# A two-layer decoder step on one core: the mixer norm's shift moved into the last down product, pools that wait tile by tile, another division of the down projection

## The chip, the cores and the metric

The kernel runs on one core of a Trainium2 chip. The metric is the device time of one launch in microseconds (us); the kernel before takes 1140.86 us (median of three runs, 1140.83 to 1141.41). Engines are named as the profile names them: PE is the matrix engine (PEld its weight loads, which overlap the products), DVE the vector engine, ACT the scalar engine, POOL the GpSimd engine, SP the engine that only issues transfers. "POOLq", "DVEq" and the like are the instruction queues of these engines. Transfers issued by POOL form a DMA queue of their own.

## The reference

One step of a two-layer decoder, width 1024, for a prompt of 512 rows and 8 sample rows. Layer 0 mixes the rows by sliding-window attention, layer 1 by gated linear attention. Behind each mixer, and behind each feed-forward part, stands a layer norm of ALPHA·x + f(x). Cut to what the change touches:

```python
xp = layer_norm(ALPHA * xp + mp, ln_mix_g[i], ln_mix_b[i])   # mixer norm
fp, cp = conv_ffn(xp, buf0, ffn_w_up[i], ffn_conv_w[i], ffn_conv_b[i], ffn_w_down[i])
xp = layer_norm(ALPHA * xp + fp, ln_ffn_g[i], ln_ffn_b[i])   # ffn norm

def layer_norm(x, g, b):
    mu = mean(x); var = mean((x - mu) ** 2)
    return (x - mu) * rsqrt(var + LN_EPS) * g + b

def conv_ffn(x, buf, w_up, conv_w, conv_b, w_down):
    h = x @ w_up                              # 1024 -> 2 x 2816
    a, u = h[..., :D_FF], h[..., D_FF:]
    ap = concatenate([buf, a], axis=1)
    c = conv_b + sum(conv_w[j] * ap[:, j:j + T] for j in range(3))
    y = (gelu(c) * u) @ w_down                # 2816 -> 1024
    return y, ap[:, T:]
```

## The kernel before

**Data.** Activations are kept transposed: 128 of the 1024 features on the partitions, eight such blocks (KD), the rows of the batch along the free axis. The 520 rows are two groups, a (256 prompt rows) and b (256 prompt rows and the 8 samples). A 32-bit product is made of three products in the reduced 32-bit type: every operand is split into a high and a low half, and high·high, high·low and low·high are summed in PSUM. One "unit" is a weight tile of 128 x 1024 with its halves wh and wl; a unit's product for one group is 24 matmuls.

**Weights.** SP loads a unit into `raw`; ACT rounds it to wh. The low half is made in one of two ways. Either DVE subtracts, wl = raw - wh (L192); or, in `low_by_dma` (L195), ACT writes wl = -wh (L197) and a transfer issued by POOL adds the weights from memory to it (L198). Six slots (WSLOTS) hold wh and wl; a product that is done releases its slot, and the next load is issued there.

**Feed-forward.** The 22 blocks of 128 hidden features (j = 0 to 21) run in two manners. Blocks 0 to 3 are a gate unit and a value unit each (`ffn_gate`, `ffn_value`), group by group. Meanwhile `row_sums` (L445) prepares sums and differences of the groups' rows, and from block 4 on (PAIRED) `ffn_pair` computes gate and value of both groups together by seven half products (named a11, a12, s2, s1, a22, s4, s3) of 12 matmuls each, 84 in all, in "wide" PSUM tiles of two banks, except the first, a11, in a one-bank tile `onep`. DVE recombines the results (L821), convolves, and splits the gated product into hh, hl (hs for group a), the operands of the down projection.

**The mixer norm's shift.** The norm's result is x·g·r + b. The rounded operands xh, xl get the bias at once, but x itself, which the residual needs later, gets it by a pass of its own: `shift` (L439, the instruction is L441) on POOL, one per group and block, 16 per layer. For the mixer norms these passes are issued by `row_sums` and kept in program order; the difference of the sample columns (`tsum`, L483 and L484) is taken from the shifted x behind them. The norm behind the first feed-forward part shifts in the same way, in another place.

**Down.** The hidden blocks are gone through in parts, FF_PARTS: three of 4 blocks by pairs of output blocks between the pairs (`ffn_down2`, 48 matmuls a unit, 16 units in all with the fourth part), each adding onto x, and the last part of six blocks behind the last pair by `ffn_down`, one unit (18 matmuls a group) for each of the eight output blocks. There four "heads" in four PSUM banks first take the five blocks that are ready (60 matmuls), and then the sixth. `ln_chunk` adds each result to x (L322) and begins the following norm: after output block 0, ones x x gives a first mean (`sc`, L328), which DVE and POOL subtract from all blocks (L337); squares and sums are gathered by POOL (L354, L355).

**What sets the order.** The Tile framework schedules all instructions with a model of the engines and issues them in that order on each engine; an engine runs its queue strictly in order. `issue_after` and `keep_in_program_order` are constraints on that schedule. PSUM is switched at the first pair (L813) from the pools mps and acc to one and wide, and back after the last pair; a pool that opens in space that another leaves waits for all of that pool's tiles.

## Time and profile before

| what | value |
|---|---|
| device time, median of 3 | 1140.86 us (1140.83 to 1141.41) |
| profiled execution | 1140.54 us, of which the span (first to last instruction) 1138.8 us |
| PE busy | 1079.0 us, 95% |
| DVE, ACT, POOL busy | 898.1, 655.3, 339.0 us (79, 58, 30%) |
| mean granted clock of PE | 0.982 |

Stages of the span by their times: the attention layer's products up to 187 us; its feed-forward blocks 0 to 3 to about 221.6; the opening of the pairs to 241; the pairs of layer 0 to 486.3; its last down part and norm to 561; the linear attention to about 787.6; blocks 0 to 3 of layer 1 to 817; the opening to 841; the pairs to 1085.9; the last down part, norm and output to the end. In a row of the windows view the columns are: window, its length, then for PE, PEld, DVE, ACT and POOL the busy time with the count of instructions, the granted clock of PE, the busy share of the DMA engines, and GB/s. In the waits view: who waits, for what, us in total, times, longest. In the timeline: start, duration, engine, line and operation, and in brackets an idle time before it with what ended it; a row can stand for several instructions (x7).

### The profile page before, as it was taken

Reading aid. Unit: us, or ns where it says so; the run is one execution under the profiler, and the core shown is the slowest. Engines: PE = TensorE matmul, PEld = TensorE weight load, DVE = VectorE, ACT = ScalarE, POOL = GpSimd, SP = SyncE. Lnnn points to the kernel's source line nnn. Section 1 sums busy time; section 2 is a strip of 40 time slices with the busy share of each in tenths; the row PEclk is TensorE's granted clock in tenths of the full one; section 3 lists DMA queues with packets and bytes.
Section 4 is the critical chain, followed back from the end, with each engine's and each line's share of the span. In section 5 each row is a group of like instructions: output and inputs, shape, how many; then the busy total and the mean of one; then the engine's idle time right before and its main releaser. Section 6 shows DMA issues by size and latency. Waiting matters only on the chain.

```text
span 1138.8 us, 23875 instructions
## 1 busy us (share of the span) xinstructions
PE 1079.0 (95%) x9174; PEld 1044.8 (92%) x9174; DVE 898.1 (79%) x1796; ACT 655.3 (58%) x1307; POOL 339.0 (30%) x567
## 2 busy tenths in 40 slices
PE   8998999799999999999999999998799999999995
PEld 8997898699999999988899899898799999999985
DVE  7897669957888778877867787779978887877866
ACT  5677556755556665535545555456665566566534
POOL 3575574611111111056311100373411111111045
PEclk9999999989999999999899999999999999999998
DMA  7553034657777777332134454444567777777312
GB/s 227 152 179 101 13 100 130 162 149 177 180 181 174 178 174 183 98 95 91 55 108 130 125 187 144 140 123 148 143 154 185 173 181 173 179 185 179 96 49 76
DMA packets 64465, 161.68 MB, mean 142 GB/s; under 512 B 7992, under 2 KB 28512, under 8 KB 64352
## 3 DMA queue, kind: packets, MB, share of 16 engines
q1 hardware_dynamic: 51536, 119.47, 32.9%
q0 software_dynamic: 10656, 38.80, 19.8%
q10 hardware_dynamic: 2160, 1.89, 0.5%
q8 instruction: 72, 1.18, 0.4%
q14 instruction: 41, 0.34, 0.1%
HBM read 147.47 MB, written 8.47 MB: 137 GB/s over the span
## 4 chain that ended last, share of the span: by engine, by line
PE 57%; DVE 12%; DMA 5%; POOL 3%; issue 2%; ACT 2%; SPq 0%; ACTq 0%; DVEq 0%; POOLq 0%
PE widep L295 8%; PE widep L296 8%; PE widep L297 8%; PE widep L885 5%; PE widep L884 5%; PE widep L883 5%; DMA vb<-dv 3%; PE accp L230 3%; PE accp L228 3%; PE accp L232 3%; PE onep L297 1%; PE onep L296 1%; PE onep L295 1%; DVE xs_a L427 1%; POOL x_a L337 1%
## 5 line engine op out<-in xcount | busy, mean ns | idle before, releaser
L300 ACT ACTIVATE wh<-raw 128x1024 fp32r<-128x1024 f32 x72 | 76.6, 1064 | 119.5 <-PE widep L884 84.4
L198 POOL DMA_DIRECT2D wl<-in_w_down x32 | 27.6, 864 | 338.2 <-ACT wl L197 337.8
L186 ACT ACTIVATE wh<-raw 128x1024 fp32r<-128x1024 f32 (+2 forms) x96 | 97.2, 1012 | 53.5 <-PE widep L296 19.1
L228 PE MATMUL accp<-xh_b,wh 128*128 128x264 f32 x400 | 114.6, 287 | 11.8 <-DVE hprod L797 8.7
L295 PE MATMUL widep<-th,wh 128*128 128x264 f32 (+1 forms) x432 | 119.4, 276 | 0.0
L296 PE MATMUL widep<-tl,wh 128*128 128x264 f32 (+1 forms) x432 | 119.4, 276 | 0.0
L297 PE MATMUL widep<-th,wl 128*128 128x264 f32 (+1 forms) x432 | 119.2, 276 | 0.0
L228 PE MATMUL accp<-xs_a,wh 128*128 128x256 f32 x400 | 110.6, 291 | 2.8 <-ACT xs_a L426 1.1
L232 PE MATMUL accp<-xh_b,wl 128*128 128x264 f32 x400 | 112.6, 281 | 0.0
L230 PE MATMUL accp<-xl_b,wh 128*128 128x264 f32 x384 | 108.1, 282 | 0.0
L230 PE MATMUL accp<-xs_a,wh 128*128 128x256 f32 x384 | 105.2, 287 | 0.2
L301 DVE TENSOR_TENSOR wl<-raw,wh 128x1024 fp32r<-128x1024 f32 x72 | 88.0, 1222 | 19.9 <-ACT wh L300 19.9
L228 PEld LDWEIGHTS accp<-xh_b,wh 128*128 128x128 f32 x400 | 76.5, 191 | 14.4 <-DVE hprod L797 9.7
L821 DVE TENSOR_TENSOR merged<-widep,conv 128x528 f32<-128x528 f32 x72 | 37.4, 561 | 65.0 <-PE widep L297 65.0
L228 PEld LDWEIGHTS accp<-xs_a,wh 128*128 128x128 f32 x400 | 79.1, 198 | 4.9 <-ACT xs_a L426 1.3
L295 PEld LDWEIGHTS widep<-th,wh 128*128 128x128 f32 x432 | 82.4, 191 | 0.0
L296 PEld LDWEIGHTS widep<-tl,wh 128*128 128x128 f32 x432 | 82.4, 191 | 0.0
L297 PEld LDWEIGHTS widep<-th,wl 128*128 128x128 f32 x432 | 82.3, 191 | 0.0
L192 DVE TENSOR_TENSOR wl<-raw,wh 128x1024 fp32r<-128x1024 f32 (+3 forms) x64 | 75.3, 1182 | 7.2 <-ACT wh L186 6.6
L295 PE MATMUL widep<-xh_b,wh 128*128 128x264 f32 x288 | 79.6, 276 | 0.0
L296 PE MATMUL widep<-xl_b,wh 128*128 128x264 f32 x288 | 79.5, 276 | 0.0
L297 PE MATMUL widep<-xh_b,wl 128*128 128x264 f32 x288 | 79.5, 276 | 0.0
(420 smaller groups left out, 4282.4 us busy)
## 6 DMA issues: line engine op xcount, KB each, us to landing
raw<-in_w_up SPq DMA_DIRECT2D x88, 512.0 KB, 3.6
wl<-in_w_up POOLq DMA_DIRECT2D x42, 512.0 KB, 6.3
raw<-in_w_down SPq DMA_DIRECT2D x32, 512.0 KB, 4.1
wl<-in_w_down POOLq DMA_DIRECT2D x32, 512.0 KB, 6.3
raw<-in_w_gla SPq DMA_DIRECT2D x24, 512.0 KB, 3.6
raw<-in_w_mix_o SPq DMA_DIRECT2D x16, 512.0 KB, 4.3
raw<-in_w_down SPq DMA_DIRECT2D x16, 384.0 KB, 3.1
qs<-hl SPq DMA_DIRECT2D x64, 64.0 KB, 2.2
```

Of the source, the lines that this page charges most:

```text
L186: nc.scalar.activation(h[:, c], r[:, c], AF.Copy)
L192: nc.vector.tensor_tensor(l[:, c], r[:, c], h[:, c].bitcast(F32), op=ALU.subtract)
L228: nc.tensor.matmul(o, h[:, ks], xh, start=k == 0, stop=False)
L230: nc.tensor.matmul(o, h[:, ks], xl, start=False, stop=False)
L232: nc.tensor.matmul(o, l[:, ks], xh, start=False, stop=not tail and k == nt - 1)
L295: self.nc.tensor.matmul(o, h[:, ks], rh, start=k == 0, stop=False)
L296: self.nc.tensor.matmul(o, h[:, ks], rl, start=False, stop=False)
L297: self.nc.tensor.matmul(o, l[:, ks], rh, start=False, stop=k == KD // 2 - 1)
L300: self.nc.scalar.activation(hi, src, AF.Copy)
L301: self.nc.vector.tensor_tensor(lo, src, hi.bitcast(F32), op=ALU.subtract)
L883: nc.tensor.matmul(o, h[:, ks], rh, start=k == 0, stop=False)
L884: nc.tensor.matmul(o, h[:, ks], rl, start=False, stop=False)
```

## The change

1. **Shift.** In `row_sums` the 16 shifts are gone. A tile `back` holds ALPHA·b, made by one POOL instruction in `ffn_open`, and the last down product's addition to x becomes x + back + ps in one instruction. `tsum` moves ahead of the first sums; since x is unshifted there, the difference of the biases (`step`) is added by two more small instructions.
2. **Pools.** All pools that open and close in the middle of the kernel, in PSUM and in SBUF, wait tile by tile (`reuse_waits="tile"`).
3. **Parts.** The last two parts of FF_PARTS are (12, 14) and (14, 22) in place of (12, 16) and (16, 22). A part of two blocks covers four output blocks per unit, so that a unit is 48 matmuls as before; there are 14 units between the pairs in place of 16, and the pairs 18 to 21 follow each other with none between. The last part has eight blocks: units of 512 KB and 24 matmuls a group.
4. **Last down's low halves.** `ffn_down` joins the units whose low halves are made by ACT and a transfer from POOL's queue.
5. **Heads.** Two heads (FULL) take all three products of the seven ready blocks, two take only the products with wh, and their low products come last. The heads are issued behind the last pair's last matmul.
6. **Order of the first pairs.** a11 of the pairs 4 to 6 is issued behind the last matmul written before it, and in pair 4 the product a22 goes ahead of s1.

The number of matmuls of the whole kernel's products is unchanged by 3 and 5.

```diff
-FF_PARTS = ((0, 4), (4, 8), (8, 12), (12, 16), (16, 22))
+FF_PARTS = ((0, 4), (4, 8), (8, 12), (12, 14), (14, 22))
+ORDERED = 3
+FULL = 2
...
     def open(self, name, bufs=1):
-        cm = self.tc.tile_pool(name=name, bufs=bufs)
+        cm = self.tc.tile_pool(name=name, bufs=bufs, reuse_waits="tile")
...
     def psum(self, name, bufs=1):
-        cm = self.tc.tile_pool(name=name, bufs=bufs, space=PSUM)
+        cm = self.tc.tile_pool(name=name, bufs=bufs, space=PSUM, reuse_waits="tile")
...
-            if self.units[u][2] in (self.ffn_down2, self.ffn_gate, self.ffn_value):
+            if self.units[u][2] in (self.ffn_down2, self.ffn_down, self.ffn_gate, self.ffn_value):
                 self.low_by_dma(l[:, c], h[:, c], src[:, c])
...
         if scaled:
-            nc.vector.tensor_tensor(x[:, m], x[:, m], ps, op=ALU.add)
+            nc.vector.scalar_tensor_tensor(x[:, m], x[:, m], self.back[:, m:m + 1], ps, op0=ALU.add, op1=ALU.add)
...
+        ts = self.pp.tile([P, 2, half, NS], F32, name="tsum")
+        gap = step.unsqueeze(2).broadcast_to([P, half, NS])
+        for q, x, y, op in ((0, lo, hi, ALU.subtract), (1, hi, lo, ALU.add)):
+            v.tensor_tensor(ts[:, q], b.x[:, x, 256:], b.x[:, y, 256:], op=ALU.subtract)
+            v.tensor_tensor(ts[:, q], ts[:, q], gap, op=op)
+            self.split(self.th[q][:, :, :, n:], self.tl[q][:, :, :, n:], even(ts[:, q]))
...
-        for m in (*range(half, KD), *range(half)):
-            yield 1
-            for g in (b, a):
-                self.shift(g, i, m)
-        ts = self.pp.tile([P, 2, half, NS], F32, name="tsum")
-        v.tensor_tensor(ts[:, 0], b.x[:, lo, 256:], b.x[:, hi, 256:], op=ALU.subtract)
-        v.tensor_tensor(ts[:, 1], b.x[:, hi, 256:], b.x[:, lo, 256:], op=ALU.subtract)
-        for q in range(2):
-            self.split(self.th[q][:, :, :, n:], self.tl[q][:, :, :, n:], even(ts[:, q]))
...
+        b0 = C_LNB + 2 * layer * KD
+        g.tensor_scalar(self.back, self.par[:, b0:b0 + KD], ALPHA, 0.0, op0=ALU.mult, op1=ALU.add)
...
-        self.half_product(p1, W["a11"], part(a, lo), n)
+        with self.tc.issue_after(self.final) if j < PAIRED + ORDERED else ExitStack():
+            self.half_product(p1, W["a11"], part(a, lo), n)
...
+        products = [(p[:, 0], W["s1"], t1, m), (p[:, 1], W["a22"], t4, n)]
+        for x in reversed(products) if j == PAIRED else products:
+            self.half_product(*x)
...
-            self.heads = heads[2:] + heads[:2]
-            for i, ps in enumerate(self.heads):
-                self.down_steps(g, u + i, ps, range(end))
+            self.heads = [self.acc.tile([P, 512], F32, name="accp") for _ in range(HEADS)]
+            with self.tc.issue_after(self.final):
+                for i, ps in enumerate(self.heads):
+                    self.down_steps(g, u + i, ps, range(end), range(end) if i < FULL else (), True, False)
         if g.i == 0 and m < HEADS:
             ps = self.heads[m]
-            self.down_steps(g, u, ps, [end])
+            self.down_steps(g, u, ps, [end], [end] if m < FULL else range(end + 1), False, True)
```

How the order on the engines moves, at three places. First POOL's queue at the opening of layer 0's pairs, before the change (aext is the gate's convolution input, nconv_p and sconv the convolution state that is written out):

```order
L198 DMA wl<-in_w_down 128x1024
L441 TENSOR_SCALAR x_b<-x_b,par 128x264
L441 TENSOR_SCALAR x_a<-x_a,par 128x256
...
L304 COPY aext<-hist 128x2
L198 DMA wl<-in_w_up 128x1024
L304 COPY nconv_p<-aext 128x2
```

and with it:

```order
L312 COPY aext<-hist 128x2
L201 DMA wl<-in_w_down 128x1024
L201 DMA wl<-in_w_up 128x1024
L312 COPY nconv_p<-aext 128x2
L312 COPY sconv<-aext 128x8
L500 TENSOR_SCALAR xl_b<-xl_b 128x8x4
```

Between the low halves of the first down unit and those of pair 5's first tile (in_w_up) stood 16 shifts, of which the first two are shown; now nothing stands there.

Second, PE at the same place, before (onep_3606 is a11 of pair 5, whose low half is wl_3345; accp_3349 is the last value product; widep_3428 is a12 of pair 4):

```order
L230 MATMUL accp_3349<-xl_b_90,wh_3019 128x264
L232 MATMUL accp_3349<-xh_b_89,wl_3020 128x264
L295 MATMUL onep_3606<-xs_a_86,wh_3344 128x256
L296 MATMUL onep_3606<-xs_a_86,wh_3344 128x256
L297 MATMUL onep_3606<-xs_a_86,wl_3345 128x256
...
L295 MATMUL widep_3428<-xs_a_86,wh_3096 128x256
L296 MATMUL widep_3428<-xs_a_86,wh_3096 128x256
L297 MATMUL widep_3428<-xs_a_86,wl_3097 128x256
```

and with the change (accp_3337 is the last value product, onep_3401 a11 of pair 4, widep_3416 its a12):

```order
L233 MATMUL accp_3337<-xl_b_91,wh_3030 128x264
L235 MATMUL accp_3337<-xh_b_90,wl_3031 128x264
L303 MATMUL onep_3401<-xs_a_87,wh_3103 128x256
L304 MATMUL onep_3401<-xs_a_87,wh_3103 128x256
L305 MATMUL onep_3401<-xs_a_87,wl_3104 128x256
...
L303 MATMUL widep_3416<-xs_a_87,wh_3103 128x256
L304 MATMUL widep_3416<-xs_a_87,wh_3103 128x256
L305 MATMUL widep_3416<-xs_a_87,wl_3104 128x256
```

Before, a11 of pair 5 stood ahead of pair 4's wide products (a11 of pair 4 was further up, ahead of the last value product). Now a11 of pair 4 follows the last value product, and a11 of pair 5 comes behind the whole of pair 4 and the 48 matmuls of the first down unit.

Third, POOL's queue behind the last pair of layer 0, before (sb is the first mean of the norm, s_a and s_b the sums of squares):

```order
L337 TENSOR_TENSOR x_a<-x_a,sb 128x256 x7
L355 TENSOR_TENSOR s_a<-s_a,sq 128x256 x3
L337 TENSOR_TENSOR x_b<-x_b,sb 128x264 x7
L354 TENSOR_TENSOR s_b<-x_b 128x264
L355 TENSOR_TENSOR s_b<-s_b,sq 128x264
L958 MEMSET wh 128x1024
```

and with it:

```order
L345 TENSOR_TENSOR x_a<-x_a,sb 128x256 x7
L363 TENSOR_TENSOR s_a<-s_a,sq 128x256 x3
L201 DMA wl<-in_w_down 128x1024
L345 TENSOR_TENSOR x_b<-x_b,sb 128x264 x7
L362 TENSOR_TENSOR s_b<-x_b 128x264
L363 TENSOR_TENSOR s_b<-s_b,sq 128x264
L201 DMA wl<-in_w_down 128x1024
L969 MEMSET wh 128x1024
```

The low halves of the seventh and the eighth unit of the last down part, subtractions on DVE before, are transfers that POOL issues behind the norm's subtractions; those of the first six are issued ahead of them. Layer 1's tail has the same order.

More of the change, by code (lines that the diff above doesn't have):

```diff
@@ L119, in __init__ @@
         nc.gpsimd.memset(self.eps[:, 1:2], 1.0)
+        self.back = c.tile([P, KD], F32, name="back")
         for i, g in enumerate(self.groups):
@@ L235, in product, with place @@
             nc.tensor.matmul(o, w[:, k * P:(k + 1) * P], in_turn(r[:, k]), start=False, stop=k == nt - 1)
+        self.final = self.nc.cur_bb.bb.instructions[-1]
         return ps[:, :g.n]
+    @staticmethod
+    def place(j):
+        return (j - FF_PARTS[-1][0]) % HSLOTS
     def pair_tasks(self, u):
@@ L874, in ffn_down2 @@
         j0, j1 = FF_PARTS[part]
-        for g in self.groups:
+        nk = j1 - j0
+        ms = KD // nk
+        for g, m in ((g, ms * i + m) for g in self.groups for m in range(0, ms, 2)):
             ps, n = self.wide(), g.n
@@ L878, in ffn_down2 @@
                 o = ps[:, s, :n].rearrange("p (j t) -> p j t", t=2)
-                for k in range(j1 - j0):
-                    t, q = s * (j1 - j0) + k, (j0 + k) % HSLOTS
+                for k in range(nk):
+                    t, q = (m % ms + s) * nk + k, self.place(j0 + k)
                     ks = slice(t * P, t * P + P)
@@ L891, in ffn_down2, with down_steps @@
         self.release()
-    def down_steps(self, g, u, ps, ks):
+    def down_steps(self, g, u, ps, highs, lows, first, last):
         nc = self.nc
         h, l = self.w[u]
-        o, end = ps[:, :g.n].rearrange("p (j t) -> p j t", t=2), self.units[u][1] - 1
-        for k in ks:
-            w = slice(k * P, k * P + P)
-            rh, rl = in_turn(g.hh[:, k]), in_turn(g.hl[:, k])
-            nc.tensor.matmul(o, h[:, w], rh, start=k == 0, stop=False)
-            nc.tensor.matmul(o, h[:, w], rl, start=False, stop=False)
-            nc.tensor.matmul(o, l[:, w], rh, start=False, stop=k == end)
+        o = ps[:, :g.n].rearrange("p (j t) -> p j t", t=2)
+        both = set(highs) & set(lows)
+        steps = [(l, g.hh, k) for k in lows if k not in both]
+        for k in highs:
+            steps += [(h, g.hh, k), (h, g.hl, k)] + [(l, g.hh, k)] * (k in both)
+        for n, (w, r, k) in enumerate(steps):
+            nc.tensor.matmul(o, w[:, k * P:(k + 1) * P], in_turn(r[:, k]), start=first and n == 0, stop=last and n == len(steps) - 1)
     def ffn_down(self, g, u, layer, part, m):
@@ L1202, in plan @@
             last = len(FF_PARTS) - 1
[L1203 to L1210 removed]
+            downs = [(part, i) for part, (j0, j1) in enumerate(FF_PARTS[:last]) for i in range(j1 - j0)]
+            for j in range(NF):
+                q = self.place(j)
+                if j < PAIRED:
                     first = (lambda layer=layer: self.ffn_open(layer)) if j == 0 else None
@@ L1213, in plan @@
                     add(I["w_up"][layer, 2 * j + 1], KD, self.ffn_value, layer, j, q)
+                    continue
+                add((I["w_up"][layer, 2 * j], I["w_up"][layer, 2 * j + 1]), KD, self.ffn_pair, layer, j, q)
+                if downs and FF_PARTS[downs[0][0]][1] <= j:
+                    part, i = downs.pop(0)
+                    add(I[f"w_down{part}"][layer, i], KD, self.ffn_down2, layer, part, i)
+            j0, j1 = FF_PARTS[last]
             for m in range(KD):
```

22 lines of the change are left out of this document (6 added, 16 removed).

## The prediction

> **What bounds the kernel now.** I read the page's busy times first, then the windows by stage, then the waits of PE, and last the timelines of single engines at the places that the waits named.
>
> ```profile
> PE 1079.0 (95%) x9174; PEld 1044.8 (92%) x9174; DVE 898.1 (79%) x1796; ACT 655.3 (58%) x1307; POOL 339.0 (30%) x567
> ```
>
> ```profile
> 187.00:221.60 34.60, 30.77 (x254) 29.18 (x254) 33.52 (x74) 26.47 (x49) 15.94 (x27) 1.00 0.62 164
> 221.60:241.24 19.64, 12.15 (x83) 12.15 (x83) 7.78 (x18) 6.89 (x14) 4.77 (x14) 0.74 0.36 86
> 241.24:486.30 245.06, 245.04 (x2186) 244.84 (x2184) 199.35 (x338) 147.53 (x216) 31.87 (x65) 1.00 0.71 169
> 486.30:524.00 37.70, 34.88 (x297) 34.14 (x297) 26.82 (x50) 16.01 (x33) 27.52 (x41) 1.00 0.30 93
> 817.20:840.85 23.65, 17.09 (x133) 16.74 (x133) 18.17 (x33) 12.75 (x26) 6.59 (x18) 0.93 0.46 115
> 840.85:1085.90 245.05, 245.04 (x2186) 244.84 (x2184) 199.75 (x338) 147.52 (x216) 31.90 (x65) 1.00 0.70 169
> 1085.90:1117.50 31.60, 28.45 (x237) 27.77 (x238) 20.76 (x38) 11.53 (x23) 18.23 (x23) 1.00 0.10 32
> ```
>
> PE is the bound: in the two stages of pairs it works 245.04 of 245 us at full clock, 2186 matmuls, or 0.112 us each. No matmul is removed, so the change can only take PE's idle and slow stretches, and of those it touches four: the two openings of the pairs (221.6 and 817) and the two last down parts (486 and 1086).
>
> ```profile
> PE onep L297 <- DMA wl<-in_w_up: 9.0, 2, 7.5
> PE accp L228 <- DVE hprod L797: 8.7, 5, 4.7
> PE accp L900 <- DVE merged L821: 3.6, 2, 2.0
> PE accp L232 <- DVE wl L192: 2.6, 3, 1.4
> ```
>
> These four lines, 23.9 us together, name what PE waits for there: a low half that comes by DMA, the gated product hprod, the last pair's recombination, a low half that DVE makes.
>
> **Layer 0's opening.**
>
> ```profile
> 221.60:229.05 7.45, 0.00 (x0) 0.00 (x0) 5.19 (x14) 2.81 (x8) 4.46 (x11) 0.72 0.48 80
> 229.05:235.06 6.01, 5.97 (x28) 5.97 (x29) 0.00 (x0) 1.06 (x1) 0.13 (x2) 0.50 0.20 76
> ```
>
> ```profile
> 217.70 1.06 ACT L197 ACTIVATE wl<-wh 128x1024 fp32r<-128x1024 f32 x1
> 223.27 0.48 POOL L441 TENSOR_SCALAR x_a<-x_a,par 128x256 f32<-128x256 f32 x1
> 223.87 0.78 POOL L198 DMA_DIRECT2D wl<-in_w_up  x1
> DMA to landing us min/median/max: 5.2/6.3/9.2
> L441 POOL TENSOR_SCALAR x_b<-x_b,par x24: 475/502/1551, 212.1 to 820.2; 128x264 f32<-128x264 f32 x24
> L441 POOL TENSOR_SCALAR x_a<-x_a,par x24: 468/478/1527, 212.8 to 820.7; 128x256 f32<-128x256 f32 x24
> ```
>
> Pair 5's a11 stands in PE's queue ahead of pair 4's wide products, and its low half is late: ACT's part was done at 218.8, but POOL issued the transfer at 223.87, behind the last shift, and 5.2 us later, at 229.05, PE went on. PE lost 7.45 us, and then ran 28 matmuls in 6.01 us at half the granted clock, where 28 x 0.112 = 3.1 would do: 2.9 more. That is 10.35 us. The change takes the cause away twice: no shifts ahead of the transfer, and a11 of pair 5 only behind pair 4 and a down unit (84 + 48 matmuls, 14.8 us later), when the transfer has long landed.
>
> What is late next is the last hprod. In the order of the change, the last value product and a11 of pair 4 follow each other, then pair 4's second wide tile takes banks that the last value product held, so it waits until DVE has read them.
>
> ```profile
> 216.07 0.89 DVE L246 TENSOR_TENSOR sum<-raw 128x512 f32<-128x512 f32 x1 [0.56 <-DMA raw<-in_w_up]
> 221.02 0.42 DVE L797 TENSOR_TENSOR hprod<-conv,accp 128x264 f32<-128x264 f32 x1
> 223.32 0.46 DVE L483 TENSOR_TENSOR tsum<-x_b 128x32 f32<-128x32 f32 x1 [1.89 <-POOL x_b L441]
> 227.66 0.42 DVE L797 TENSOR_TENSOR hprod<-conv,accp 128x264 f32<-128x264 f32 x1
> ```
>
> Before, the last hprod ran only at 227.66, among 14 DVE instructions after the 1.89 us in which tsum waited for a shift. Without that wait, and with tsum done earlier, I move it forward by some 5 us, to 222–223, against PE's last value product at about 221.2 and the 36 matmuls (4 us) of a11, a12 and s2 that cover it in part. But the sum of pair 4's weights (L246 here) stands ahead of an hprod on DVE and waits for a load, and tsum has two instructions more (under 0.5 us each by the L483 row). I charge 1.1 us for these two and for tsum's split, 0.9 for a stall behind the sum, 0.5 for the second wide tile: 2.5. Bounds: no new wait, a gain of 10.35; a wait as long as the longest hprod wait of the list, 4.7, a gain of 5.65. I take 10.35 - 2.5 = **7.9**, because the new waits have their data within 2 us of need by these rows.
>
> **Layer 1's opening.**
>
> ```profile
> 813.81 7.64 DVE L780 SCALAR_TENSOR_TENSOR conv<-aext,par,conv 128x256 f32<-128x256 f32 x1
> L780 DVE SCALAR_TENSOR_TENSOR conv<-aext,par,conv x16: 472/485/7639, 176.7 to 830.6; 128x256 f32<-128x256 f32 x16
> 821.84 0.38 PE L228 MATMUL accp<-xh_b,wh 128*128 128x264 f32 x1 [4.70 <-DVE hprod L797]
> 817.00:821.80 4.80, 0.14 (x2) 0.00 (x0) 4.78 (x2) 0.31 (x1) 4.36 (x11) 1.00 0.58 119
> 821.80:825.60 3.80, 3.76 (x18) 3.76 (x19) 3.71 (x8) 3.40 (x7) 0.10 (x1) 0.55 0.26 91
> PE onep L297 <- DMA wl<-in_w_up: 1.5, 1, 1.5
> ```
>
> One DVE instruction that takes 485 ns in the median took 7.64 us, and it ended, at 821.4, with the shifts (the last one starts at 820.7 by the row of L441; POOL is busy 4.36 of the 4.80 us before). DVE's next instruction is the hprod that PE waited for. I read this as DVE and POOL keeping each other from memory: as long as POOL had shifts in its queue, the DVE instruction did not go through. The Trainium skill says of this ("SBUF — State Buffer", section "SBUF: two separate sides") that DVE and GpSimd share a port pair as an exclusive lock which one holds for a whole instruction while the other fully blocks. By its words one shift, not fourteen, would be waited for; the trace goes further than the page.
>
> The shifts gone, 4.70 goes, the slow clock behind it (18 matmuls in 3.80 us where 2.0 would do, 1.8), and the 1.5 of the low half: 8.0. Against that I set waits of the kind of layer 0's, 1.9. **6.1**; bounds 8.4 (with a 0.4 us wait of a wide product too) and 1.9 (the long instruction stays, so that 4.70 and 1.8 stay).
>
> **Pairs.** Two units of 48 matmuls leave this stage in each layer, and their 96 return in the last part, which has eight blocks in place of six for 16 products of group and output block: PE's sum is the same. Pairs 18 to 21 in a row give DVE less cover. In the pair stage DVE is busy 199.35 of 245.06 us; were all of it the 18 pairs' own, it would be 11.1 us a pair, against 84 x 0.112 = 9.4 of PE, so that DVE could fall at most 4 x 1.7 = 6.8 us behind in four pairs. It holds the down units' additions too, the weights of pairs 18 and 19 are prepared during 16 and 17, between which units still stand, and DVE loses eight low halves at this end. I take **0**, with bounds 0 and +6.8 a layer. The pools' tile-by-tile waits are fewer waits at the same places, and cost nothing.
>
> **Last down part, layer 0.**
>
> ```profile
> PE accp L232 <- DVE wl L192: 0.6, 1, 0.6
> 488.23 0.35 PE L900 MATMUL accp<-hs_a,wh 128*128 128x256 f32 x1 [1.95 <-DVE merged L821]
> 496.35 0.70 PE L328 MATMUL sc<-x_a,ones_a 128*128 128x256 f32 x2
> 497.56 5.83 POOL L337 TENSOR_TENSOR x_a<-x_a,sb 128x256 f32<-128x256 f32 x7 [2.20 <-ACT sb L330]
> 503.35 3.12 POOL L355 TENSOR_TENSOR s_a<-s_a,sq 128x256 f32<-128x256 f32 x3
> 506.46 6.64 POOL L337 TENSOR_TENSOR x_b<-x_b,sb 128x264 f32<-128x264 f32 x7
> L198 POOL DMA_DIRECT2D wl<-in_w_down x32: 856/862/899, 211.5 to 1046.5; - x32
> ```
>
> Gains: the heads waited 1.95 for the last recombination because all wide tiles had to be free; tile by tile the first head's bank was read earlier. The wait for a low half by DVE (0.6) goes with the subtractions. The heads' more matmuls (80 in place of 60) cover the gated product's way to hs. Losses: POOL's queue. sc ran at 496.35, and the seventh unit's transfer stands behind the x_a and s_a rows: issued at 506.5, 10.1 us behind sc, landed by the shortest landing, 5.2, 15.4 behind sc. PE reaches that low half after about 115 matmuls, 13 us behind sc: 2.3 late, say **+2.2**. The eighth stands behind x_b (6.64) and two sums (0.74 and 0.93 in the same timeline): 19.2 behind sc, landed 24.5; PE, with 70 more matmuls and the 2.2, is there at 23: **+1.3**. The following norm of group a is covered by 85 matmuls in place of 92: **+0.6**. Together -1.95 - 0.6 + 2.2 + 1.3 + 0.6 = **+1.5**. Bounds: -2.6 (transfers in time), and +10 (both landings at 9.2, and a stretch at half clock, 2.9 as above).
>
> The Trainium skill speaks against this step in the same section: a transfer issued from GpSimd's queue can starve for descriptors while DVE holds the port. It gives about 0.62 us alone and 3.1 beside such DVE work. By that figure the two late transfers of a layer would cost, as an estimate from that page, 2.5 us more each, +10 in both layers, and the sum below would be 1139. The rows say otherwise so far: 32 issues in 856 to 899 ns, beside a DVE that was 81% busy.
>
> **Last down part, layer 1.**
>
> ```profile
> PE accp L900 <- DVE merged L821: 1.7, 1, 1.7
> PE accp L232 <- DVE wl L192: 1.4, 1, 1.4
> ```
>
> These are the same two waits there: -1.7 and -1.4, +2.2 and +0.9 for the two transfers, and the last norm ends the kernel, so its 0.6 counts in full: **+0.7**, with bounds -3.1 and +9.
>
> **Sum.** -7.9 - 6.1 + 1.5 + 0.7 = -11.8. The profiled execution took 1140.54 us (span 1138.8 and 1.7 around it): 1128.7; the median of the runs shown is 0.3 above it, so **1129**.
>
> **The rivals.**
>
> *A new bound in the openings* (14%). DVE, not POOL, holds hprod back once the shifts are gone: it is busy 33.52 of 34.60 us in 187 to 221.6. For it speaks that row; against it that its queue there waited for shifts and loads, which are gone or early. Each opening then keeps a wait of 4.7 and a part of the slow clock: gains 4.7 and 3.0 in place of 7.9 and 6.1, so 1140.9 - 7.7 + 2.2 = 1135.4.
>
> *The long L780 is not the shifts' doing* (8%). If DVE could lose only one POOL instruction, at most 1.55 us by the L441 row, layer 1 keeps 4.7 - 1.55 and the slow clock, and gains 1.7 in place of 6.1: 1133.4. This is what the lock of the SBUF page taken at its word gives. Against it: it ended as the shifts ended. That the change doesn't do what it says would show in the same way, with shifts gone and the wait still there.
>
> *POOL's queue in the last down parts* (10%), the slower side. The transfers of the heads' low halves too are POOL's now, three in a row. If landing takes 9.2 in place of 5.2 to 6.3, then the heads wait 2.9, the seventh and eighth 2.9 more each, and a wait over 4 us brings 2.9 of half clock: 11.6 a layer, 23 in two. 1129 + 23 = 1152, slower than before. It decides from 5.9 us a layer beyond my sum on, half of 11.8. For it: the longest landing exists; against it: DMA is 0.30 and 0.10 busy in those windows, and most landings are at 6.3.
>
> *DVE bounds pairs 18 to 21* (6%): two thirds of the 6.8, +4.5 a layer, 1138. For it the 11.1 against 9.4; against it that pairs 20 and 21 follow each other now, at a PE of 100%.
>
> **How the numbers follow.** The forecast has 62%, and of itself lies between 1121 and 1134. Gains of both openings at their upper bounds and transfers in time would give 1140.9 - 24.4 = 1116.5, and I leave a small share below 1121. The other cases lie at 1133 to 1138 and 1152; to reach all but a tenth above, the range goes to 1138.5: **1121 to 1138.5**. What can be told from no change is 0.2%, 2.3 us: faster means under 1138.6. Faster: forecast, both opening rivals almost whole, half of the DVE rival and little of POOL's, 86%; within 0.2%: 5%; slower: 9%.
>
> **What would show it.** In the profile of the changed kernel the waits list has no 7.5 us for wl of in_w_up, no DVE instruction of L780's kind over 2 us, and clock 1.00 or nearly so in the openings, which are shorter by about 8 and 6 us. The pair stages stay at 100%. In the last down parts PE waits about 2 and 1.3 us for DMA at wl of in_w_down in each layer, and no longer for the last recombination. I am wrong if hprod waits of 4 us or more stay in the openings, if the DMA waits of the last parts reach 6 us a layer, or if PE has gaps between pairs 18 and 21.

## The result, and the profile after

The changed kernel takes 1127.99 us (median of four runs, 1127.19 to 1132.14) beside 1140.84 for the kernel before on the same chip: a ratio of 0.9895, 95% interval 0.987 to 0.9919, so 12.0 us faster by the ratio, with an interval of 9.2 to 14.8. The forecast was 1129 us, 11.8 faster.

The page of the changed kernel, its busy times:

```profile
PE 1072.6 (95%) x9174; PEld 1039.3 (92%) x9174; DVE 872.6 (77%) x1784; ACT 664.6 (59%) x1315; POOL 335.7 (30%) x549
```

PE has the same 9174 matmuls in 6.4 us less of busy time: they ran less at a slow clock. The waits view, the rows that answer to the four of before:

```profile
PE accp L913 <- DMA wl<-in_w_down: 7.7, 6, 1.5
PE accp L235 <- DMA wl<-in_w_down: 4.6, 4, 2.7
PE accp L231 <- DVE hprod L804: 4.6, 3, 2.0
PE widep L303 <- DVE hprod L804: 0.5, 1, 0.5
```

The 9.0 us of waits for in_w_up at a11 are gone, and so are the 4.7 for hprod and the 3.6 for the last recombination. The hprod waits that remain in that row (4.6, three times) stand in blocks 0 to 3, as before. New are ten waits for in_w_down, 12.3 us, all in the last down parts: 6.9 us in layer 0 and 5.4 in layer 1.

To see where the time went, both traces are cut at the same matmuls: in a layer's blocks 0 to 3, at a12 of pair 5, at the last pair's end, in blocks 0 to 3 of layer 1, and so on. The windows view of the kernel before, cut there:

```profile
0.00:194.44 194.44, 182.13 (x1534) 168.84 (x1535) 153.51 (x396) 122.52 (x356) 111.24 (x187) 0.98 0.44 132
194.44:246.62 52.18, 42.30 (x343) 41.39 (x341) 39.01 (x83) 31.21 (x53) 21.64 (x41) 0.90 0.54 134
246.62:486.28 239.66, 239.66 (x2138) 239.46 (x2136) 194.18 (x329) 144.87 (x212) 29.98 (x61) 1.00 0.70 168
486.28:799.42 313.14, 299.23 (x2409) 282.16 (x2409) 240.49 (x525) 161.34 (x382) 101.05 (x144) 0.98 0.39 122
799.42:846.23 46.81, 38.30 (x313) 37.23 (x313) 40.85 (x73) 29.88 (x50) 17.12 (x39) 0.96 0.61 149
1085.89:1138.80 52.91, 37.76 (x309) 36.29 (x308) 35.45 (x69) 20.66 (x43) 27.97 (x36) 0.94 0.18 60
```

and of the changed kernel:

```profile
0.00:192.81 192.81, 179.61 (x1534) 166.91 (x1535) 154.58 (x399) 122.70 (x356) 111.86 (x188) 1.00 0.45 133
192.81:236.06 43.25, 40.74 (x343) 40.14 (x342) 37.59 (x82) 31.87 (x54) 10.71 (x25) 0.96 0.66 164
236.06:464.96 228.90, 228.90 (x2044) 228.90 (x2042) 186.91 (x319) 140.12 (x206) 31.34 (x61) 1.00 0.69 168
464.96:792.71 327.75, 308.89 (x2506) 292.17 (x2504) 237.52 (x529) 170.17 (x395) 104.40 (x150) 0.98 0.46 132
792.71:831.45 38.74, 36.15 (x313) 35.41 (x313) 32.70 (x69) 30.29 (x48) 13.48 (x23) 1.00 0.70 172
1060.36:1126.50 66.14, 49.43 (x404) 46.83 (x403) 34.85 (x69) 28.19 (x52) 30.98 (x42) 0.95 0.49 124
```

The 96 matmuls that each layer moves from the pairs to the last down part are 10.7 us; with these put back, the differences are:

| stretch | predicted | measured in the two profiles |
|---|---|---|
| up to blocks 0 to 3 of layer 0 | 0 | 192.81 - 194.44 = -1.6 |
| opening, layer 0 | -7.9 | 43.25 - 52.18 = -8.9 |
| pairs, layer 0 | 0 | 228.90 + 10.7 - 239.66 = 0 |
| last down part to layer 1's blocks 0 to 3 | +1.5 | 327.75 - 10.7 - 313.14 = +3.9 |
| opening, layer 1 | -6.1 | 38.74 - 46.81 = -8.1 |
| pairs, layer 1 | 0 | 228.91 + 10.7 - 239.66 = 0 |
| last down part, layer 1, to the end | +0.7 | 66.14 - 10.7 - 52.91 = +2.5 |
| sum | -11.8 | -12.3 |

Of the edits only part 2 reaches into the first row. Its clock is 0.98 before and 1.00 after in these two executions. `dve_lows` below, which has part 2 as well, takes 194.47 us there, as long as the kernel before, so I count the 1.6 us as scatter and not as a gain.

In the last down parts the larger waits are these (the timeline of PE, rows with an idle time, others between them left out; layer 0, then the first two of layer 1):

```profile
466.72 0.38 PE L913 MATMUL accp<-hs_a,wl 128*128 128x256 f32 x1 [1.54 <-DMA wl<-in_w_down]
470.19 0.38 PE L913 MATMUL accp<-hs_a,wl 128*128 128x256 f32 x1 [1.08 <-DMA wl<-in_w_down]
477.80 0.60 PE L913 MATMUL accp<-hs_a,wl 128*128 128x256 f32 x3 [1.10 <-DMA wl<-in_w_down]
479.83 0.60 PE L913 MATMUL accp<-hs_a,wh 128*128 128x256 f32 x3 [1.43 <-ACT hs_a L308]
485.21 0.58 PE L235 MATMUL accp<-hs_a,wl 128*128 128x256 f32 x1 [2.67 <-DMA wl<-in_w_down]
...
1061.51 0.38 PE L913 MATMUL accp<-hs_a,wl 128*128 128x256 f32 x1 [0.94 <-DMA wl<-in_w_down]
1065.39 0.38 PE L913 MATMUL accp<-hs_a,wl 128*128 128x256 f32 x1 [1.50 <-DMA wl<-in_w_down]
```

The waits for DMA are at the heads' units and at the fifth. Of the two units that the prediction charged, the seventh has 0.52 and 0.16 us in the two layers and the eighth has no wait. The row of 479.83 is a wait of another kind, for the last gated product. ACT makes it, and ACT's own timeline has it idle for 3.31 and 2.10 us just before, until late loads of raw weights (at 471.24 and 475.11), and then writing two -wh, ahead of that work. The windows view of the two stretches from the last pair to sc, and the landing row of POOL's transfers, show what the DMA engines did:

```profile
464.96:481.72 16.76, 11.61 (x97) 10.85 (x96) 6.30 (x12) 8.67 (x13) 5.35 (x14) 1.00 1.04 264
1060.36:1076.02 15.66, 11.61 (x97) 10.85 (x96) 6.24 (x12) 7.85 (x11) 3.80 (x6) 1.00 1.05 277
DMA to landing us min/median/max: 5.1/6.5/11.5
```

The last two columns are the share of the DMA engines and GB/s. Every unit is now read twice, by the load and by the transfer that adds to -wh. The DMA engines are full in these stretches (1.04, 1.05), and the transfers issued for them take 6.2 to 11.5 us to land; before, 9.2 was the most of the whole kernel.

### The profile page after: what moved, and what is told of

It is laid out like the page before. It is cut to its first block, busy times and chain, and to the rows that moved or that the text cites. A ratio compares the mean times of both kernels' runs of the same rounds, so it can differ in the third digit from the quotient of the medians.

```text
span 1126.5 us, 23813 instructions
## 1 busy us (share of the span) xinstructions
PE 1072.6 (95%) x9174; PEld 1039.3 (92%) x9174; DVE 872.6 (77%) x1784; ACT 664.6 (59%) x1315; POOL 335.7 (30%) x549
## 4 chain that ended last, share of the span: by engine, by line
PE 60%; DVE 17%; DMA 10%; ACT 6%; issue 4%; POOL 2%; SPq 0%; ACTq 0%; DVEq 0%; POOLq 0%
PE widep L303 7%; PE widep L304 7%; PE widep L305 7%; PE accp L233 5%; PE accp L231 5%; PE accp L235 5%; PE widep L895 4%; PE widep L894 4%; PE widep L896 4%; DMA raw<-in_w_down 2%; DMA wl<-in_w_down 2%; DMA vb<-dv 2%; DVE wl L195 1%; PE onep L304 1%; PE onep L303 1%
## 5 line engine op out<-in xcount | busy, mean ns | idle before, releaser
L189 ACT ACTIVATE wh<-raw 128x1024 fp32r<-128x1024 f32 (+1 forms) x92 | 96.3, 1048 | 68.4 <-PE accp L233 31.7
L201 POOL DMA_DIRECT2D wl<-in_w_down x44 | 38.0, 864 | 311.8 <-ACT wl L200 307.4
L200 ACT ACTIVATE wl<-wh 128x1024 fp32r<-128x1024 f32 x86 | 90.1, 1050 | 0.9
```

Source lines behind the costliest of these rows:

```text
L189: nc.scalar.activation(h[:, c], r[:, c], AF.Copy)
L200: self.nc.scalar.activation(l, h.bitcast(F32), AF.Copy, scale=-1.0)
```

## The experiments

Twelve kernels were run. Ratios are to the kernel before on the same chip, with their 95% intervals; comparisons between them go by the ratios, and 0.01 is 11.4 us. The first four test what made the openings long and what the last down parts lost; after the fourth, `dve_lows`, had come out far below both kernels, the others start from it.

| run | median, us | ratio (95%) |
|---|---|---|
| changed kernel | 1127.99 | 0.9895 (0.987 to 0.9919) |
| shift_only: before + part 1 | 1133.64 | 0.9937 (0.9913 to 0.9961) |
| order_only: before + part 6 | 1139.60 | 0.9995 (0.9977 to 1.0013) |
| dummies: changed + idle passes | 1135.80 | 0.9950 (0.9927 to 0.9973) |
| dve_lows: changed - part 4 | 1110.86 | 0.9736 (0.9714 to 0.9757) |
| dummies2: dve_lows + idle passes | 1117.89 | 0.9812 (0.9795 to 0.9829) |
| late_dma: dve_lows + part 4 for units 7, 8 | 1121.32 | 0.9836 (0.9821 to 0.9850) |
| head_dma: dve_lows + part 4 for units 1 to 4 | 1119.57 | 0.9830 (0.9809 to 0.9850) |
| parts_back2: dve_lows - part 3 | 1121.75 | 0.9840 (0.9825 to 0.9855) |
| pools_off2: dve_lows - part 2 | 1123.33 | 0.9857 (0.9841 to 0.9874) |
| order_off2: dve_lows - part 6 | 1123.99 | 0.9873 (0.9852 to 0.9893) |
| shift_back2: dve_lows - part 1 | 1123.15 | 0.9861 (0.9844 to 0.9878) |
| best: dve_lows, heads rearranged | 1110.14 | 0.9761 (0.9729 to 0.9793) |

**shift_only: the shift alone.**

```diff
 # before, with part 1 of the change: no shift passes, `back`, the earlier tsum
-        for m in (*range(half, KD), *range(half)):
-            yield 1
-            for g in (b, a):
-                self.shift(g, i, m)
+            nc.vector.scalar_tensor_tensor(x[:, m], x[:, m], self.back[:, m:m + 1], ps, op0=ALU.add, op1=ALU.add)
```

> The kernel before with part 1 alone (no shift passes, ALPHA times the bias added with the last down product, tsum earlier; the scratch tile of ffn_open shares hprod's space as in the change). Theory (the shifts hold back both POOL's transfer and DVE): both openings gain most of the 17 us that they gained in the change (8.9 and 8.1), less 2 to 3 us because a11 of pair 5 still stands ahead of pair 4's wide products and its low half lands near 224; the last down parts stay as before. 1125 to 1128 us. Rival (the order of the first pairs is what counts): layer 0 keeps most of its stall, 1132 us or more.

1133.64 us, a ratio of 0.9937: 7.2 us gained. That is less than the theory asked and in the range of the rival. Its row in the waits view:

```profile
PE onep L298 <- DMA wl<-in_w_up: 8.5, 2, 4.4
```

PE still reaches pair 5's a11 ahead of pair 4's wide products, and its low half is 4.4 and 4.1 us late in the two openings, although no shift stands before its transfer. The shifts made this wait longer in layer 0 (7.5 with them); they were not its only cause. Both theories had a part of it.

**order_only: the order of the first pairs alone.**

```diff
+        with self.tc.issue_after(self.final) if j < PAIRED + ORDERED else ExitStack():
+            self.half_product(p1, W["a11"], part(a, lo), n)
...
+        for x in reversed(products) if j == PAIRED else products:
+            self.half_product(*x)
```

> The kernel before with part 6 alone (a11 of the first three pairs behind the matmul written before it, a22 ahead of s1 in pair 4); the shifts stay. Theory: the 7.5 us wait for the low half moves away, but the last hprod of layer 0 comes as late as before (227.7 by the trace of before), so that PE waits some 4 us for it with the wide tiles, and the stretched DVE instruction and the 4.7 us behind it stay in layer 1: 1136 to 1139 us. Rival (order alone cures layer 0): 10 us less, 1131.

1139.60 us, 0.9995: no difference that can be told, and 0.6 us above the theory's range. The waits view has

```profile
PE widep L297 <- DVE hprod L799: 14.3, 2, 7.2
```

The wait for the low half went, and a wait for the last hprod of 7.1 to 7.2 us took its place in each opening, since the first wide tile of a pool that waits as a whole has to wait for it. How much of hprod's lateness is the shifts' this run doesn't show: `pools_off2` below, without shifts, has 4.1 and 6.7 us at the same place. So part 1 alone and part 6 alone give 7.2 and 0.6 us; in the changed kernel the openings gave 17.0.

**dummies: passes that nobody waits for.**

```diff
+        for m in (*range(half, KD), *range(half)):
+            yield 1
+            for g in (b, a):
+                self.tc.keep_in_program_order(nc.gpsimd.tensor_scalar(g.x[:, m], g.x[:, m], 1.0, 0.0, op0=ALU.mult, op1=ALU.add))
```

> The changed kernel with 16 passes per layer of the shift's size added at the shift's place, x times 1 plus 0, in place on POOL; nothing reads their results until the down products much later, and tsum stays ahead of them. Theory (POOL's stream of passes locks DVE out): a DVE instruction of over 5 us appears again in an opening, hprod is late, 1134 to 1139 us. Rival (what cost time was that tsum and the transfer waited for the shifts): within 2 us of the changed kernel, 1128 to 1130.

1135.80 us, within the range of the first theory, but nine of its ten runs are spread from 1130.14 to 1141.77 (the tenth took 1223.96), no DVE instruction in an opening is over 1.6 us in the profiled one, and at pair 4 PE waits only 1.9 and 0.4 us for hprod. What that execution lost against the changed kernel, 5.0 us, stands in layer 1's last down part. So this run did not decide, and it was repeated without part 4's transfers beside it:

**dummies2: the same passes, by the same lines, in dve_lows.**

> The version with DVE's subtractions (dve_lows, 1110.9) with the 16 idle passes per layer of the dummies run, to see their price without the last down parts' late transfers beside them. Theory A (POOL's passes lock DVE out by themselves): 1116 us or more, with hprod waits of several us or a DVE instruction over 5 us in an opening. Theory B (what cost time before were the instructions that waited for the passes: tsum in DVE's queue ahead of hprod, and the transfer in POOL's queue): 1111 to 1113 us.

1117.89 us, 0.9812 in place of 0.9736: 8.7 us, as theory A asked. The timeline of DVE and of POOL in layer 1's opening (rows of the first and the last passes), and PE's row there:

```profile
795.17 4.20 DVE L490 SCALAR_TENSOR_TENSOR raw<-x_b,step 128x256 f32<-128x256 f32 x3
799.29 3.53 DVE L791 SCALAR_TENSOR_TENSOR conv<-aext,par,conv 128x256 f32<-128x256 f32 x1
```

```profile
796.08 0.74 POOL L495 TENSOR_SCALAR x_b<-x_b 128x264 f32<-128x264 f32 x1
...
802.06 0.48 POOL L495 TENSOR_SCALAR x_a<-x_a 128x256 f32<-128x256 f32 x1
802.96 0.19 POOL L312 COPY aext<-hist 128x2 f32<-128x2 f32 x1 [0.41 <-DVE conv L791]
```

```profile
803.21 0.59 PE L231 MATMUL accp<-xh_b,wh 128*128 128x264 f32 x1 [4.85 <-DVE hprod L808]
```

Nothing waits for the passes' results, and yet between the first pass (796.1) and the last one's end (802.5) DVE worked at two instructions only: the third L490, which took 3.4 us of the 4.20, and the L791 of 3.53. PE stood 4.85 us for the hprod behind them. That is the row of 7.64 us of the kernel before again, in two pieces. Theory A stands: the passes hold DVE back by themselves. They did so in layer 1's opening; in layer 0's, no DVE instruction beside the passes is over 1.3 us.

**dve_lows: DVE makes the last part's low halves again.**

```diff
-            if self.units[u][2] in (self.ffn_down2, self.ffn_down, self.ffn_gate, self.ffn_value):
+            if self.units[u][2] in (self.ffn_down2, self.ffn_gate, self.ffn_value):
```

> The changed kernel without part 4: the last down part's low halves are DVE's subtractions again. Theory (the last down parts lost 3.9 and 2.5 us to six waits of PE for low halves that were still on their way, since loads and transfers overlapped and landed in 7 to 10 us): those 12 us of waits fall to 3 or 4 us, raw loads land earlier, 1122 to 1125 us. Rival (eight subtractions of 1.2 us in DVE's queue, just when it recombines the last pairs, delay hs and the norm by as much): 1127 to 1130.

1110.86 us: 18 us below the changed kernel by the ratios, and 11 below what the theory asked. The windows of the same stretches (last pair of layer 0 to the blocks of layer 1; layer 1's last down part to the end), then those from the last pair to sc and from sc to the norm of group a, and the largest wait of the heads:

```profile
465.88:780.98 315.10, 305.02 (x2506) 289.06 (x2504) 247.54 (x537) 166.08 (x389) 103.44 (x144) 0.99 0.40 125
1049.61:1109.60 59.99, 48.21 (x404) 46.58 (x403) 41.50 (x76) 24.96 (x48) 27.91 (x36) 0.93 0.23 75
465.88:479.19 13.31, 11.38 (x98) 10.84 (x96) 10.39 (x18) 6.04 (x9) 1.88 (x10) 1.00 0.63 208
479.19:502.15 22.96, 22.96 (x203) 22.84 (x202) 16.68 (x28) 9.07 (x18) 19.76 (x22) 1.00 0.23 72
```

```profile
PE accp L913 <- DVE merged L828: 1.6, 1, 1.6
```

With the 96 matmuls put back, the two stretches are 315.10 - 10.7 - 313.14 = -8.8 and 59.99 - 10.7 - 52.91 = -3.6 us against the kernel before, where the changed kernel has +3.9 and +2.5. So part 4 cost 12.7 and 6.1 us, and the other parts together gained 8.8 and 3.6 in these stretches. From sc to the norm of group a PE runs without a gap. The waits for DMA that vanished are 12.3 of the 18.8 us. A part of the rest is known: the 1.43 us for hs, and 3.4 us at half the granted clock (0.50 in 485.01 to 488.42 of the changed kernel, 1.00 here). The row of the heads' wait shows something that the changed kernel hid: in layer 0, 1.6 us of the wait for the last recombination are still there with tile-by-tile pools.

**late_dma: part 4 for the seventh and eighth unit alone.**

```diff
-            if self.units[u][2] in (self.ffn_down2, self.ffn_gate, self.ffn_value):
+            if self.units[u][2] in (self.ffn_down2, self.ffn_gate, self.ffn_value) or (self.units[u][2] == self.ffn_down and self.units[u][3][-1] >= 6):
```

> dve_lows with the low halves of the seventh and eighth unit of the last down part alone made by ACT and POOL's transfer. The prediction's term (these two stand behind the norm's subtractions in POOL's queue and come 2.2 and 1.3 us late in layer 0, 2.2 and 0.9 in layer 1): waits for wl of in_w_down appear at these two units, 1115 to 1118 us. Theory from the changed kernel's profile (the waits come from the DMA engines being full when all eight units are both loaded and added to): with two transfers they are not full, 1111 to 1113 us.

1121.32 us, 0.9836: 11.4 us more than dve_lows, above what either theory asked. The waits view, the timeline of POOL and DVE behind sc in layer 0, and the window behind it:

```profile
PE accp L235 <- DMA wl<-in_w_down: 5.2, 4, 1.7
```

```profile
486.29 2.35 POOL L363 TENSOR_TENSOR s_a<-s_a,sq 128x256 f32<-128x256 f32 x3
488.71 0.88 POOL L201 DMA_DIRECT2D wl<-in_w_down  x1
489.32 5.23 POOL L345 TENSOR_TENSOR x_b<-x_b,sb 128x264 f32<-128x264 f32 x7
...
498.14 0.88 POOL L201 DMA_DIRECT2D wl<-in_w_down  x1 [0.42 <-ACT sq L350]
```

```profile
489.67 5.16 DVE L362 TENSOR_TENSOR s_a<-s_a,x_a 128x256 f32<-128x256 f32 x1
```

```profile
509.71:529.27 19.56, 18.51 (x133) 17.20 (x132) 15.38 (x30) 10.46 (x20) 8.43 (x12) 0.91 0.22 75
```

The prediction's mechanism is here as it was written: the two transfers stand behind POOL's norm work, sc being at 479.38: issued 9.3 and 18.8 us behind it (10.1 and 19.2 predicted). PE waits for them 5.2 us in both layers together (6.6 predicted). But that is less than half of the price. The trace adds a DVE instruction of the norm stretched to 5.16 us beside the seven subtractions of POOL, once in each layer, where dve_lows has none of this kind over 0.9 us. The window of clock 0.91 is not shown to come from the late transfers: 3.4 us of it are at half clock (521.22 to 524.64), 17 us behind the last of the two waits. PE's order differs here from that of dve_lows (241 and 203 matmuls between sc and group a's norm), so the stretches behind sc can't be set against each other one by one. How the 11.4 us divide is not shown. The DMA engines were not full here (0.65 and 0.56 from the last pair to sc, 0.41 and 0.20 behind it), and the four transfers landed in 5.3 to 5.7 us: these units are late by their place in POOL's queue.

**head_dma: part 4 for the heads' units alone.**

```diff
-            if self.units[u][2] in (self.ffn_down2, self.ffn_gate, self.ffn_value):
+            if self.units[u][2] in (self.ffn_down2, self.ffn_gate, self.ffn_value) or (self.units[u][2] == self.ffn_down and self.units[u][3][-1] < 4):
```

> dve_lows with the low halves of the first four units of the last down part (the heads' ones) alone made by ACT and POOL's transfer. Theory (loads and transfers together fill the DMA engines, busy 1.04 of the window in the changed kernel, so that a transfer lands 7 to 10 us after its issue): the heads wait some 1 us at two or three low halves a layer, 1113 to 1116 us. Rival (the late units behind the norm's subtractions are the whole price of part 4): 1110 to 1112 us.

1119.57 us, 0.9830, 10.7 us more than dve_lows, and more than the theory asked. Its waits, and the window from layer 0's last pair to sc:

```profile
PE accp L913 <- DMA wl<-in_w_down: 6.7, 6, 2.3
465.21:482.37 17.16, 13.33 (x98) 12.37 (x96) 8.54 (x14) 7.54 (x12) 3.61 (x12) 0.90 0.94 246
```

The DMA engines are at 0.94 there, and 0.87 in layer 1, beside 0.63 and 0.55 in dve_lows, and the heads' transfers take 7.4 to 11.5 us to land. So the early units alone cost as much as the late ones, by another mechanism, and the rival that put the whole price on the late ones falls. The two prices, 11.4 and 10.7, make 22.1 together, against 18.1 for all eight units: a part of them overlaps. In the changed kernel PE waited 2.67 and 1.23 us at the fifth unit and then came to the seventh and eighth when they had all but landed.

**parts_back2: six blocks in the last part.**

```diff
-FF_PARTS = ((0, 4), (4, 8), (8, 12), (12, 14), (14, 22))
+FF_PARTS = ((0, 4), (4, 8), (8, 12), (12, 16), (16, 22))
```

> dve_lows with the old parts, (12, 16) and (16, 22): six blocks in the last part. Theory (the longer last part covers the way of the last hs and the norm of group a; against the kernel before, the last down parts of dve_lows are 9 and 4 us shorter, more than the 2.6 and 3.1 us of waits there, because stretches at a slow clock went too): 1117 to 1121 us. Rival (the tile-by-tile pools and the heads alone do it): 1110 to 1113 us.

1121.75 us, 0.9840: 11.9 us more, a little above the theory's range and far from the rival's. The wait for DVE's low halves is back, and it is the smaller part of the price; layer 0's window from group a's norm to group b's has a PE that stands at times and a slow clock again, as before the change:

```profile
PE accp L235 <- DVE wl L195: 2.8, 4, 1.4
504.49:525.63 21.14, 19.69 (x139) 18.03 (x138) 18.59 (x34) 10.27 (x23) 12.23 (x17) 0.92 0.26 78
```

The same window of dve_lows (502.15 to 520.95) has 161 matmuls in 18.80 us, without a gap and at 1.00: 22 matmuls more in 2.3 us less.

**pools_off2: pools that wait as a whole.**

```diff
-        cm = self.tc.tile_pool(name=name, bufs=bufs, space=PSUM, reuse_waits="tile")
+        cm = self.tc.tile_pool(name=name, bufs=bufs, space=PSUM)
```

and the same for the pools in SBUF.

> dve_lows with pools that wait as a whole. Theory: the heads wait again for the last recombination, about 2 us a layer, and the first pair's wide tiles for the last hprod, 1 to 2 us a layer, 1115 to 1119 us. Rival (nothing on the path): 1110 to 1112 us.

1123.33 us, 0.9857: 13.8 us more, above the theory's range. Its waits, from an execution that took 1130.62 us, the longest of the five, so that they may be longer than usual:

```profile
PE widep L303 <- DVE hprod L804: 10.8, 2, 6.7
PE accp L913 <- DVE merged L828: 6.9, 2, 3.4
```

At the first pair PE waits 4.1 and 6.7 us for the last hprod before any wide tile may be written; tile by tile it waits 0.5 at most in the changed kernel and 1.5 in dve_lows, behind 36 matmuls. The heads wait 3.4 in each layer.

**order_off2 and shift_back2: dve_lows without part 6, and without part 1.**

```diff
-        with self.tc.issue_after(self.final) if j < PAIRED + ORDERED else ExitStack():
-            self.half_product(p1, W["a11"], part(a, lo), n)
+        self.half_product(p1, W["a11"], part(a, lo), n)
...
-        for x in reversed(products) if j == PAIRED else products:
+        for x in products:
```

> dve_lows without part 6: a11 of the first pairs may be hoisted and s1 comes ahead of a22 again; shifts gone, pools tile by tile. Theory (a11 of pair 5 stands ahead of pair 4's wide products and its low half lands some 4 us after PE gets there, as in shift_only, whose waits were 4.4 and 4.1 us): 1118 to 1122 us. Rival (without the shifts the transfer is in time): 1110 to 1112 us.

```diff
-            nc.vector.scalar_tensor_tensor(x[:, m], x[:, m], self.back[:, m:m + 1], ps, op0=ALU.add, op1=ALU.add)
+            nc.vector.tensor_tensor(x[:, m], x[:, m], ps, op=ALU.add)
...
+        for m in (*range(half, KD), *range(half)):
+            yield 1
+            for g in (b, a):
+                self.shift(g, i, m)
```

> dve_lows without part 1: the shift passes and the late tsum are back, all other parts stay. Theory (the idle passes alone cost 7.0 in dummies2; tsum's wait for the last pass in DVE's queue, ahead of the last hprod, comes on top, as in order_only with its two hprod waits of 7 us): 1121 to 1126 us. Rival (the passes cost what the idle ones cost): 1117 to 1119 us.

1123.99 us (0.9873, 15.6 us more, above the theory's range) and 1123.15 us (0.9861, 14.3 more, as the theory asked). The first waits for the low half of pair 5, the second for the sample columns, the tsum that stands behind the last shift; rows of the two waits views:

```profile
PE onep L305 <- DMA wl<-in_w_up: 9.8, 2, 5.8
```

```profile
PE widep L302 <- ACT th L307: 4.8, 2, 2.6
PE widep L303 <- DVE tl L308: 3.4, 2, 1.7
```

The shift passes cost 14.3 us, the idle passes 8.7. The difference of 5.6 us has an interval of about 3 us to either side, so shifts that something waits for cost more than idle passes. The waits differ too: here PE waits 8.2 us for the sample columns and has no hprod wait over 2.0 us, where dummies2 has the 4.85. So one wait stands in place of the other rather than on top of it.

**best: the heads rearranged.**

```diff
-FULL = 2
+FULL = 4
...
+            self.heads = [heads[i] for i in (0, 2, 3, 1)]
```

> dve_lows with all four heads complete (84 matmuls before the last block in place of 70 that were ready) and the head whose bank the last recombination frees put last. Theory: the waits of 1.6 us for that bank in layer 0 and 1.5 us for hs in layer 1 shrink to under 0.5 each: 1107.5 to 1109.5 us. Rival (the low halves of the third and fourth head are not ready yet, or the wait only changes its name): 1110 to 1113 us.

1110.14 us, 0.9761 with an interval of 0.9729 to 0.9793, which holds dve_lows' 0.9736: no gain that can be told. Its profiled execution, the longest of its runs (1116.95 us), has a wait for hprod of 4.83 us, where dve_lows and the changed kernel have 2.0 at most; two timelines, DVE's and PE's:

```profile
803.73 0.69 DVE L254 TENSOR_TENSOR sum<-raw 128x512 f32<-128x512 f32 x1 [4.69 <-DMA raw<-in_w_up]
```

```profile
812.32 0.55 PE L303 MATMUL widep<-th,wh 128*128 128x256 f32 x1 [4.83 <-DVE hprod L804]
```

It is the sum of pair 4's weights, which stands in DVE's queue ahead of the last hprod and waits for a load: what the prediction charged 0.9 us for, and what takes 4.7 when the load is late.

## Why the prediction was right, and which of its terms were not

**The openings** (-7.9 and -6.1; -8.9 and -8.1 measured). The reading was right: a transfer and a DVE instruction held by the shifts, PE's slow clock behind the waits. The charges for new waits, 2.5 and 1.9, were too high: the trace of the change has 0.5 and 0.6 us at pair 4's wide tiles. "The change takes the cause away twice" was wrong: neither edit does it alone. Without the shifts a11's low half is still 4.4 and 4.1 us late (shift_only); with the new order alone PE waits 7.1 and 7.2 us for hprod (order_only). The gain hangs on three edits at once: shift alone gave 7.2 us, order alone 0.6, and without the pools' tile-by-tile waits the openings keep 4.1 and 6.7 us. And it was fifteen shifts, not fourteen, that began while the long L780 ran.

**"The pools' tile-by-tile waits are fewer waits at the same places, and cost nothing."** As a cost this holds; as a term it failed: they are worth 13.8 us in dve_lows. The prediction let the second wide tile of pair 4 wait for hprod, and thereby used the pools' edit in the opening's sum, but it gave it no price of its own.

**The last down parts** (+1.5 and +0.7; +3.9 and +2.5 measured). Here the step that failed is the sum's choice of what is late. The gain was taken as the waits that go, 2.6 and 3.1 us, less 0.6 in each layer for the norm; without part 4 it is 8.8 and 3.6 for the other parts together. That the longer part has a share in it is seen from sc on, where PE is busy 22.96 of 22.96 us, and from parts_back2, which loses 11.9 us. The loss by the transfers was taken as 2.2 + 1.3 and 2.2 + 0.9, for the seventh and eighth unit; it is 12.7 and 6.1. The mechanism of these two units is seen by itself in late_dma, with 5.2 us of waits where 6.6 were forecast, but its price of 11.4 us is larger than its waits; in the changed kernel they cost 0.7 us of waits. The heads' units, which the prediction put into a rival with 2.9 us a layer, cost 10.7 us in all by themselves (head_dma). By the prediction's own sign it was wrong here: it named waits for DMA of 6 us a layer, and layer 0 has 6.9. The argument against that rival, that the DMA engines are 0.30 and 0.10 busy in those windows, read the profile of a kernel that reads each of these units once, over a window longer than the loads: with the change the share there is 1.04. The two mistakes have opposite signs: the losses were taken 12.2 us too low, the gains 7.9.

**Luck.** What is left of them, 4.2 us too slow, is made up by the openings, 3.0 better than forecast, and by the 1.6 us of scatter. That the time came out 1 us from the forecast is owed to these errors of opposite sign; the openings and the pairs came out as forecast, the last down parts did not. Two small sums of the prediction are off as well: layer 1's last part adds up to +0.6, not +0.7, and the gain of 1.7 in the rival of the long L780 to 1.15 by its own terms. Neither moves the range.

**The rivals.** DVE as the bound of pairs 18 to 21 did not come: 2044 matmuls in 228.90 us without a gap. A new bound in the openings did not come in the changed kernel; one execution of `best` has such a wait (4.83), behind a late load. That the stretched L780 is not the shifts' doing is refuted by dummies2. POOL's transfers in the last down parts came out at 12.7 and 6.1 us, near the 11.6 a layer that the rival was given in layer 0 and half of it in layer 1, though mostly at the heads and the fifth unit; the gains beside it hid it.

**The Trainium skill** on the shared port pair ("SBUF — State Buffer", section "SBUF: two separate sides"): that DVE and GpSimd exclude each other agrees with dummies2. By an exclusion for one instruction at a time, DVE would get in behind each pass; the traces have single DVE instructions of 7.64, 5.16 and 3.53 us beside streams of POOL instructions of 0.5 to 1 us. Its warning on transfers from GpSimd's queue was of the right direction, but the reason seen here is another. The issues for in_w_down took 828 to 893 ns, not longer than before, the four transfers of the seventh and eighth units, which the prediction's estimate was about, landed in 5.1 to 5.8 us, and those that landed late did so with the DMA engines full.

## What to carry to other kernels

A change of several parts can be right in its sum and hold a part that costs more than the whole gains: taking parts away one by one found 18 us in one line. It also found that four others are each needed by the rest: they are worth 12 to 16 us each, where two of them alone had given 7 and 1. These four prices add up to 56 us, where dve_lows gains 30 in all, so they are not shares of its gain. Part 5, the heads, was not taken away by itself. Before work is moved to a DMA queue that looks idle, the loads and the transfers of that very stretch are to be added up against the share that the window shows, since the mean over a longer window hides a burst. And a wait that is removed can be worth more than its length, where a slow clock follows it: price the stretch, not the wait.

## What the runs showed of the hardware

- A stream of short POOL passes can hold one DVE instruction for several us (7.64, 5.16 and 3.53 where 0.5 is usual), though no data ties the two. It is not always so: in order_only the 16 shifts of layer 1 took 12.6 us in place of 7.6, and no DVE instruction beside them was over 1.3 us: the two engines took turns and both were slow.
- The same wait doesn't always bring a slow clock. In pools_off2 PE waited 3.43 us at the heads of layer 0 and 3.45 at those of layer 1; the clock stayed at 1.00 behind the first and was at half for 3.4 us behind the second. Short waits did it too: behind three of 0.35, 0.18 and 0.43 us the clock was at half for 3.4 us in late_dma (0.50 in 521.22 to 524.64) and stayed at 1.00 in the changed kernel (522 to 532).
- With loads and accumulating transfers overlapping, the changed kernel's two stretches from the last pair to sc had a DMA share of 1.04 and 1.05 at 264 and 277 GB/s. The transfers of 512 KB issued for them took 6.2 to 11.5 us from issue to landing; the four of late_dma, at a share of 0.41 and 0.20, took 5.3 to 5.7.
